# Two-layer diffusion backbone on one core: layer 1's modulation moved from the first attention units into the output projection of layer 0

## The chip, the cores and the metric

The kernel runs on one core of a Trainium2 chip, in one launch. A core has five engines, each with its own queue of instructions that it works off in order: TensorE (PE; matmuls, with the weight loads shown as PEld), VectorE (DVE), ScalarE (ACT), GpSimd (POOL) and SyncE (SP, which here only issues DMAs). Matmuls read SBUF and write banks of PSUM. Instructions of different engines wait for one another by semaphores. The metric is the device time of one execution in microseconds, as the median of several runs.

## What is computed

A latent stream of 1024 tokens and a context of 256 tokens, both 1024 wide, go through two layers. Layer 0 ("even") has global attention with grouped queries and windowed attention; layer 1 ("odd") has a convolution module and neighbourhood attention. Each layer starts with a modulation, which is what the change is about:

```python
def modulation(cond, w, b):
    m = jax.nn.silu(cond) @ w + b
    return jnp.split(m, 3, axis=-1)
...
    for i in range(DEPTH):
        sh_l, sc_l, g_l = modulation(c, mod_w[i], mod_b[i])
        sh_c, sc_c, g_c = modulation(c_ctx, mod_w[i], mod_b[i])
        h_lat = rms_norm(x_lat, norm_g[i]) * (1.0 + sc_l[:, None, :]) + sh_l[:, None, :]
        h_ctx = rms_norm(x_ctx, norm_g[i]) * (1.0 + sc_c) + sh_c
        ...
        x_lat = x_lat + g_l[:, None, :] * y_lat
        if update_ctx:
            x_ctx = x_ctx + g_c * y_ctx
```

`mod_w[i]` is 1024 x 3072 in fp32, 12.6 MB for each layer. Its three parts of 1024 columns give shift (part 0), scale (part 1) and gate (part 2). Layer 0's shift and scale are needed before its first projection, its gate at the output projection of layer 0. Layer 1's shift and scale are needed where layer 0's output is normed for layer 1, its gate at the very end, for the latent tokens alone.

## The kernel before

**Matmuls.** All products are fp32 in accuracy: each operand is split into a high and a low half, and a product is three matmuls (`mm3`, L319 to L322). Weights are split as they arrive (`load_w`, L326): a DMA from SyncE (`wr`, L331), a cast on ScalarE (`wh`, L298) and a subtraction on GpSimd or VectorE (`wl`, L301).

**Layer 0.** Its heads are cut into four units, and the attention runs over them in the order 2, 3, 0, 1, each with ten blocks of queries. For a block: loads of the queries (`QH`, `QL`, L565), score matmuls for the row maxima (`mx`, L578, L590, L598) with VectorE reducing them (`mp`, L580, L591, L599), the negative maximum (`nmt`, L379) and its transpose (`trn`, L389) that VectorE writes into the queries (`QL`, L390), then score matmuls (`st`, L467, L471), exponentials on ScalarE (`pf`, L479), their split into `ph` (ScalarE, L298) and `pl` (GpSimd, for a part VectorE, L301), the products with the values (`ov`, L411 to L413), and the finish on VectorE (`r`, `rb`, `y`, L421 to L635), with the gate `gt` (L569) and the result stored to `Od` (L638).

**What runs beside the attention.** `weave` (L497) interleaves attention steps with fill steps. While a unit's attention runs, the fill is the projections of the next one (`pq`, `trk`, `pg`, with rotary on VectorE in `rt` and `pc`). The first unit's projections have no attention beside them; this stretch is called solo. During the last unit (number 1) the fill is the output projection: `out0_part` for the heads of the first two units of the order, then of the third one (`po`, TensorE; at the end of each product the update of `x` by the gate of layer 0 on VectorE, L1012, called x update below, 24 for each of these parts), with its inputs loaded by `load_oh` (`hl` from `Od`, L991). Then follow the last unit's share of it (`final_proj`) and the norm for layer 1 (`norm_h`).

**Order.** Nothing is ordered by hand: a scheduler gives each instruction the priority at which the program emits it, and `later(LATE)` (L266, `LATE` = 100) puts those inside it a little later than their place. The result is a fixed order for each engine.

**Modulation.** `mod_half_v` (L195) makes 512 columns of a part for one or both conditions. The silu of the condition stands in `csil`, one value for each row of weights. For each of the eight blocks of 128 rows of `mod_w`, the weights (128 x 512 fp32, 256 KB) are scaled by `csil` and added to an accumulator `macc` of 128 x 512: for the first block by one tensor_scalar on VectorE (L216), for the others by one scalar_tensor_tensor on VectorE (L221), or, for three of the blocks of the context condition (`MODP`, not in solo), by a product on ScalarE (L218) and an add on GpSimd (L219). At the end four matmuls with a column of ones sum each accumulator over the partitions (`trm`, L227), and VectorE adds the bias (`modT`, L228) and, for the scale, makes `gs` (L232). Layer 1 takes 80 such accumulate steps: six half parts for two conditions would make twelve accumulators, but the gate is made for one condition only, which leaves ten, of eight steps each.

`mod_steps` (L851) runs through layer 0's gate and then all of layer 1. One step of it, the weights' load with the accumulates, is taken at every tick of the projections in solo (`TICK0` = 1, loads of 512 KB into key and value buffers not yet in use) and at every third tick afterwards (`TICK1` = 3, loads of 256 KB into two `mw` buffers), so that layer 1's modulation runs in solo and beside the first two attention units.

## Time and profile before

| | us |
|---|---|
| runs | 1563.86, 1567.05, 1573.72 |
| median of the runs | 1567.05 |
| profiled execution, its span on the page | 1569.6 |
| projections of the first unit (solo) | 45 to 160 |
| attention units with layer 1's modulation | 160 to 440 |
| output projection, first two parts, beside the last unit | 701 to 836 |
| its last part and the norm | 836 to 932 |

The profiled execution lies within the runs; the page shows nothing outside its span. The stretches are read from the trace, by the first and last instructions of the lines named above. Only a wait on the engine that bounds a stretch costs time there.

### The profile page before, as it was taken

Reading aid. Unit: us, or ns where it says so; the run is one execution under the profiler, and the core shown is the slowest. Engines: PE = TensorE matmul, PEld = TensorE weight load, DVE = VectorE, ACT = ScalarE, POOL = GpSimd, SP = SyncE. Lnnn points to the kernel's source line nnn. Section 1 sums busy time; section 2 is a strip of 40 time slices with the busy share of each in tenths; the row PEclk is TensorE's granted clock in tenths of the full one; section 3 lists DMA queues with packets and bytes.
Section 4 is the critical chain, followed back from the end, with each engine's and each line's share of the span. In section 5 each row is a group of like instructions: output and inputs, shape, how many; then the busy total and the mean of one; then the engine's idle time right before and its main releaser. Section 6 shows DMA issues by size and latency. Waiting matters only on the chain.

```text
span 1569.6 us, 22251 instructions
## 1 busy us (share of the span) xinstructions
PE 1460.8 (93%) x6984; PEld 1178.9 (75%) x6984; DVE 1129.4 (72%) x2172; ACT 762.0 (49%) x1545; POOL 830.0 (53%) x762
## 2 busy tenths in 40 slices
PE   6989999998999999899999889999999999899995
PEld 1878877876888677588887568888887787677784
DVE  4898896797768677455488668999654466776776
ACT  2721354545454754655555746443343445545472
POOL 1561463555465675756545756665443333444575
PEclk9899999999999999999999989999999999799897
DMA  9548245424431225612112022214547888889632
GB/s 337 190 142 260 87 142 167 132 67 125 154 116 47 67 91 167 224 47 61 48 38 85 14 94 61 81 58 148 177 154 224 237 229 242 248 231 251 187 95 108
DMA packets 199438, 221.03 MB, mean 141 GB/s; under 512 B 18956, under 2 KB 155352, under 8 KB 199320
## 3 DMA queue, kind: packets, MB, share of 16 engines
q1 hardware_dynamic: 192656, 208.04, 43.5%
q10 hardware_dynamic: 6664, 11.57, 2.3%
q8 instruction: 55, 0.90, 0.2%
q14 instruction: 63, 0.52, 0.1%
HBM read 159.51 MB, written 60.03 MB: 140 GB/s over the span
## 4 chain that ended last, share of the span: by engine, by line
PE 65%; DVE 14%; DMA 11%; issue 4%; POOL 2%; SPq 2%; ACT 1%; ACTq 0%; DVEq 0%; POOLq 0%
PE p L322 6%; PE p L321 6%; PE p L320 6%; PE ov L411 4%; PE ov L413 4%; PE ov L412 4%; PE po L320 4%; PE po L321 4%; PE po L322 4%; PE st L467 4%; PE st L471 4%; DMA mw<-in_mod_w_dram 3%; DVE macc L221 2%; PE pq L322 2%; PE pq L321 2%
## 5 line engine op out<-in xcount | busy, mean ns | idle before, releaser
L301 POOL TENSOR_TENSOR pl<-pf,ph 128x512 fp32r<-128x512 f32 (+4 forms) x321 | 393.7, 1237 | 320.1 <-ACT ph L298 260.0
L301 POOL TENSOR_TENSOR wl<-wr,wh 128x256 fp32r<-128x256 f32 (+2 forms) x256 | 197.5, 788 | 203.1 <-ACT wh L298 192.4
L479 ACT ACTIVATE pf<-st 128x512 f32<-128x512 f32 x284 | 167.3, 597 | 177.4 <-PE st L471 138.3
L298 ACT CAST ph<-pf 128x512 fp32r<-128x512 f32 (+4 forms) x364 | 210.5, 588 | 28.9 <-PE ov L412 21.5
L298 ACT CAST wh<-wr 128x256 fp32r<-128x256 f32 (+2 forms) x264 | 102.8, 404 | 172.9 <-DMA wr<-in_ev_qkv_dram 40.4
L320 PE MATMUL p<-hh,wh 128*128 128x512 f32 x448 | 177.5, 398 | 2.9 <-DVE spk L301 1.5
L321 PE MATMUL p<-hl,wh 128*128 128x512 f32 x448 | 178.0, 398 | 0.2 <-POOL hl L301 0.2
L322 PE MATMUL p<-hh,wl 128*128 128x512 f32 x448 | 175.9, 400 | 0.1
L467 PE MATMUL st<-QH,KAt 128*128 128x512 f32 (+4 forms) x364 | 145.4, 401 | 11.4 <-ACT pf L479 9.7
L411 PE MATMUL ov<-ph,Vt 128*128 128x512 f32 (+4 forms) x364 | 143.5, 394 | 9.7 <-ACT ph L298 5.0
L413 PE MATMUL ov<-pl,Vt 128*128 128x512 f32 (+4 forms) x364 | 144.1, 396 | 6.8 <-POOL pl L301 3.6
L471 PE MATMUL st<-QL,KBt 68*128 68x512 f32 (+4 forms) x364 | 139.0, 391 | 5.8 <-DVE QL L390 5.7
L412 PE MATMUL ov<-ph,Vt 128*64 128x512 f32 (+4 forms) x364 | 140.5, 386 | 0.0
L1122 DVE SCALAR_TENSOR_TENSOR cps<-U,taps,cps 128x512 f32<-128x512 f32 x184 | 124.3, 748 | 0.0
L591 DVE TENSOR_REDUCE mp<-mx 128x1 f32<-128x512 f32 x128 | 85.7, 682 | 42.5 <-PE mx L590 41.8
L221 DVE SCALAR_TENSOR_TENSOR macc<-mw,csil,macc 128x512 f32<-128x512 f32 x107 | 94.5, 901 | 17.5 <-DMA mw<-in_mod_w_dram 16.7
L320 PEld LDWEIGHTS p<-hh,wh 128*128 128x128 f32 x448 | 84.6, 189 | 23.6 <-DVE spk L301 1.7
L321 PEld LDWEIGHTS p<-hl,wh 128*128 128x128 f32 x448 | 84.5, 189 | 20.4 <-POOL hl L301 0.6
L322 PEld LDWEIGHTS p<-hh,wl 128*128 128x128 f32 x448 | 84.8, 189 | 20.1 <-POOL wl L301 0.6
L467 PEld LDWEIGHTS st<-QH,KAt 128*128 128x128 f32 x364 | 71.2, 196 | 33.4 <-ACT pf L479 17.6
L413 PEld LDWEIGHTS ov<-pl,Vt 128*128 128x128 f32 x364 | 71.1, 195 | 32.5 <-POOL pl L301 7.8
L411 PEld LDWEIGHTS ov<-ph,Vt 128*128 128x128 f32 x364 | 71.3, 196 | 27.3 <-ACT ph L298 8.4
(277 smaller groups left out, 3546.2 us busy)
## 6 DMA issues: line engine op xcount, KB each, us to landing
mw<-in_mod_w_dram SPq DMA_DIRECT2D x34, 512.0 KB, 5.9
Q<-qs SPq DMA_DIRECT2D x40, 256.0 KB, 2.7
QH<-Q SPq DMA_DIRECT2D x80, 128.0 KB, 2.8
wr<-in_od_d_dram SPq DMA_DIRECT2D x64, 128.0 KB, 2.7
mw<-in_mod_w_dram SPq DMA_DIRECT2D x28, 256.0 KB, 3.3
wr<-in_ev_qkv_dram SPq DMA_DIRECT2D x32, 192.0 KB, 3.6
KAt<-KD SPq DMA_DIRECT2D x16, 384.0 KB, 6.2
wr<-in_od_wo_dram SPq DMA_DIRECT2D x48, 128.0 KB, 3.2
```

The costliest lines, as they stand in the source:

```text
L221: VE.scalar_tensor_tensor(t, w, csil[:, dk, q : q + 1], t, op0=ALU.mult, op1=ALU.add)
L298: SC.copy(hi, src)
L301: (GP if leng == "g" else VE).tensor_tensor(lo, src, hi.bitcast(F32), op=ALU.subtract)
L320: PE.matmul(o, lh, rh, start=first, stop=False)
L321: PE.matmul(o, lh, rl, start=False, stop=False)
L322: done[0] = PE.matmul(o, ll, rh, start=False, stop=last)
L411: PE.matmul(o, V[:, 64:192], ph[:, :n], start=(t == 0), stop=False)
L412: PE.matmul(g.ov[0:64, q0 : q0 + n], V[:, 0:64], ph[:, :n], start=False, stop=False)
L413: pvs.append(PE.matmul(o, V[:, 64:192], pl[:, :n], start=False, stop=(last and g.sink is None)))
L467: sts.append(PE.matmul(st[:, :n], KA[:, cs], g.QH[:, q0 : q0 + n], start=True, stop=False))
L471: PE.matmul(st[:, :n], KB[0:68, cs], g.QL[0:68, q0 : q0 + n], start=False, stop=True)
L479: SC.activation(pf[:, :n], st[:, :n], AF.Exp, scale=1.0 if g.bias else SCALE)
```

## The change

Layer 0's gate alone stays in `mod_steps`, at every second tick of solo, and what is left of it is run before solo ends. Layer 1's modulation moves into `mod1_steps`, in the stage of the output projection. Its weights come in 48 loads of 256 KB into five slices of 128 x 512 in turn: two in a spare key buffer (`mwk`), three in a spare value buffer (`mwv`), both free once the attention of the third unit has ended. The accumulators take two buffers (`acc1`, `sq1`) that are otherwise used later, and ScalarE's product gets a buffer of its own (`mtmp`). The parts run in the order scale, shift, gate. One step is taken at each yield of `out0` for the first two of its three parts, under `later(LATE)`, and what is left is run ahead of `final_proj`. 68 of the 80 accumulate steps are on VectorE, 12 on ScalarE and GpSimd.

```diff
-TICK0, TICK1 = (1, 3)
+TICK0, TICK2 = (2, 1)
...
-    def mod_half_v(pool, l, part, j, conds):
+    def mod_half_v(l, part, j, conds, acc, slices=None, tmp=None):
...
-            if solo[0] and dk % 2 == 0:
-                w2 = mw_tile()
...
+            if slices is None:
+                if not pre:
+                    w2 = mw_tile()
...
             else:
-                w = pool.tile([P, 512], F32, tag="mw", name=nm("mw"), bufs=MWB)
+                w = slices()
                 SY.dma_start(w, a["mod_w"][l, dk * P : (dk + 1) * P, c0 : c0 + 512])
...
-                elif dk in MODP[q] and not solo[0]:
-                    SC.activation(w, w, AF.Identity, scale=csil[:, dk, q : q + 1])
-                    GP.tensor_tensor(t, t, w, op=ALU.add)
+                elif dk in MODP[q] and slices is not None:
+                    m = tmp()
+                    SC.activation(m, w, AF.Identity, scale=csil[:, dk, q : q + 1])
+                    GP.tensor_tensor(t, t, m, op=ALU.add)
...
         def tick():
             beat[0] += 1
-            if beat[0] % (TICK0 if solo[0] else TICK1) == 0:
+            if solo[0] and beat[0] % TICK0 == 0:
                 with later(LATE):
-                    if mark[0] is None or solo[0]:
-                        next(mods, None)
-                    else:
-                        with tc.issue_after(mark[0].ins):
-                            next(mods, None)
+                    next(mods, None)
...
         def mod_steps():
-            for part in (2,):
-                for j in range(2):
-                    yield from mod_half_v(ap, 0, part, j, (0, 1))
-            for part in range(3):
-                for j in range(2):
-                    yield from mod_half_v(ap, 1, part, j, (0, 1) if part < 2 else (0,))
+            for j in range(2):
+                yield from mod_half_v(0, 2, j, (0, 1), lambda: ap.tile([P, 512], F32, tag="macc", name=nm("macc"), bufs=2))
...
+        run(mods)
         solo[0] = False
...
-        run(mods)
...
+        sp_k = a0.tile([P, NTOK], F32, tag="KB", name=nm("mwk"), bufs=2)
+        sp_v = a0.tile([P, 1920], F32, tag="V", name=nm("mwv"), bufs=2)
+        spare = [t[:, i * 512 : i * 512 + 512] for t, k in ((sp_k, 2), (sp_v, 3)) for i in range(k)]
+
+        def mod1_steps():
+
+            def acc():
+                macc[0] += 1
+                tag = ("acc1", "sq1")[macc[0] % 2]
+                return op_.tile([P, 512], F32, tag=tag, name=nm("macc"), bufs=1)
+
+            def slices():
+                spare.append(spare.pop(0))
+                return spare[-1]
+
+            macc = [0]
+            for part in (1, 0, 2):
+                for j in range(2):
+                    yield from mod_half_v(1, part, j, (0, 1) if part < 2 else (0,), acc, slices,
+                                          lambda: op_.tile([P, 512], F32, tag="mtmp", name=nm("mtmp"), bufs=1))
+
+        mods1 = mod1_steps()
...
         def out0(fs, e, c, wh, wl):
...
             for f in fs:
                 mm3(pp[:, :n], wh[f][:, es], wl[f][:, es], oh[c][0][:, f, :], oh[c][1][:, f, :], f == fs[0], f == fs[-1])
                 if f % 2 == 1:
+                    if fs != final:
+                        with later(LATE):
+                            next(mods1, None)
                     yield
...
+        run(mods1)
         fp = [final_proj(c) for c in range(3)]
```

The order that the scheduler gives changes at three places that matter below. In the listings, a row has the line, the operation, what is written and read (the names of the program with a number for the tile), and the shape. Lines of the changed kernel differ: L220 there is L221 before, L214 is L216, L227 is L228, L1025 is L1012, L590 is L591, L579 is L580, L598 is L599, L564 is L565, L637 is L638, L330 is L331, L211 is L213.

VectorE near the first row maxima of the attention, before; `macc` are the accumulators of the modulation, `mp` the row maxima, `rt` and `pc` the rotary of the next unit:

```order
L580 TENSOR_REDUCE mp_1320<-mx_1326 128x2
L221 SCALAR_TENSOR_TENSOR macc_1218<-mw_1219,csil,macc_1218 128x512
L221 SCALAR_TENSOR_TENSOR macc_1218<-mw_1243,csil,macc_1218 128x512
L828 TENSOR_TENSOR rt_331_1769<-pc_1602,k_cs 128x320 x2
L599 ISA mx_1339,mp_1320<-mx_1339,k_bm 128x256
L599 ISA mp_1320 128x1
L830 TENSOR_TENSOR pc_1602<-pc_1602,k_cs 128x2x320
L221 SCALAR_TENSOR_TENSOR macc_1218<-mw_1305,csil,macc_1218 128x512
L599 ISA mx_1342,mp_1320<-mx_1342,k_bm 128x256
```

And in the changed kernel, at the first row maxima:

```order
L579 TENSOR_REDUCE mp_1225<-mx_1227 128x2
L579 TENSOR_REDUCE mp_1225<-mx_1231 128x2
L300 TENSOR_TENSOR qs_1059<-trk_1055,qs_1059 128x384
L227 TENSOR_TENSOR modT_90<-trm_1106,modb 128x4
L598 ISA mx_1244,mp_1225<-mx_1244,k_bm 128x256
L598 ISA mp_1225 128x1
L598 ISA mx_1247,mp_1225<-mx_1247,k_bm 128x256
L598 ISA mp_1225 128x1
L341 SCALAR_TENSOR_TENSOR sg_1214<-sg_1214,pg_1184 128x256
```

The accumulates have left the place between the row maxima; only the last bias add of layer 0's gate is still there.

VectorE in the second part of the output projection, from its 25th x update on, before; `x` are the updates, `mp` the row maxima of the last unit's attention:

```order
L1012 SCALAR_TENSOR_TENSOR x_1883_7455<-po_8599,modT_90,x_1883_7455 128x256
L591 TENSOR_REDUCE mp_7952<-mx_8073 128x1
L1012 SCALAR_TENSOR_TENSOR x_1892_7482<-po_8616,modT_90,x_1892_7482 128x512
L591 TENSOR_REDUCE mp_7952<-mx_8079 128x1
L1012 SCALAR_TENSOR_TENSOR x_1901_7508<-po_8640,modT_90,x_1901_7508 128x512
L591 TENSOR_REDUCE mp_7952<-mx_8099 128x1
L1012 SCALAR_TENSOR_TENSOR x_1883_7455<-po_8670,modT_90,x_1883_7455 128x256
```

The same place in the changed kernel, from the 26th x update on:

```order
L1025 SCALAR_TENSOR_TENSOR x_1836_7249<-po_8595,modT_90,x_1836_7249 128x512
L220 SCALAR_TENSOR_TENSOR macc_7761<-mwv_7208,csil,macc_7761 128x512
L220 SCALAR_TENSOR_TENSOR macc_7760<-mwk_7207,csil,macc_7760 128x512
L1025 SCALAR_TENSOR_TENSOR x_1845_7275<-po_8621,modT_90,x_1845_7275 128x512
L590 TENSOR_REDUCE mp_7824<-mx_8002 128x1
L220 SCALAR_TENSOR_TENSOR macc_7760<-mwv_7208,csil,macc_7760 128x512
L220 SCALAR_TENSOR_TENSOR macc_7761<-mwk_7207,csil,macc_7761 128x512
L590 TENSOR_REDUCE mp_7824<-mx_8019 128x1
L220 SCALAR_TENSOR_TENSOR macc_7760<-mwv_7208,csil,macc_7760 128x512
L1025 SCALAR_TENSOR_TENSOR x_1827_7222<-po_8653,modT_90,x_1827_7222 128x256
L220 SCALAR_TENSOR_TENSOR macc_7761<-mwk_7207,csil,macc_7761 128x512
```

Between two x updates there now stand one or two accumulates, and row maxima of the attention stand behind them. Up to the 25th x update there are 29 accumulates on VectorE, from there to the 45th 35, and 4 behind.

SyncE behind the loads of the last unit's third group of queries (`Q_4`), before; `Od` is the attention's result, `hl` the input of the output projection, `wr` its weights:

```order
L565 DMA QH_7180<-Q_4_113 64x2x256 x2
L565 DMA QL_7181<-Q_4_113 64x2x256
L638 DMA Od<-y_7273 128x2x128
L569 DMA gt_7722<-G_148 128x2x128
L991 DMA hl_7507<-Od 128x2x512
L331 DMA wr_8291<-in_ev_wo_dram 128x256
L331 DMA wr_8297<-in_ev_wo_dram 128x256
```

And in the changed kernel:

```order
L564 DMA QH_6945<-Q_4_113 64x2x256 x2
L564 DMA QL_6946<-Q_4_113 64x2x256
L211 DMA mwk_7207<-in_mod_w_dram 128x512 x3
L211 DMA mwv_7208<-in_mod_w_dram 128x512 x3
L211 DMA mwk_7207<-in_mod_w_dram 128x512
L211 DMA mwv_7208<-in_mod_w_dram 128x512 x2
L330 DMA wr_8238<-in_ev_wo_dram 128x256
L211 DMA mwv_7208<-in_mod_w_dram 128x512
L330 DMA wr_8244<-in_ev_wo_dram 128x256
L637 DMA Od<-y_7038 128x2x128
```

Nine loads of modulation weights stand ahead of the projection's weights and of the next store of the attention's result.

More of the change, by code (lines that the diff above doesn't have):

```diff
@@ L51 @@
 PFB = 2
-MWB, WRB = 2, 2
+WRB = 2
 OHQ = 0
@@ L101, in tile_kernel @@
     turn = [0, 0]
-    mk, mwp, hold, layer = [0], [None], [0], [0]
+    mk, mwp, layer = [0], [None], [0]
     sts, pvs = [], []
@@ L193, in mod_half @@
                                     op0=ALU.add, op1=ALU.mult)
[L195 removed]
+    def mod_half_v(l, part, j, conds, acc, slices=None, tmp=None):
         c0 = part * 1024 + j * 512
[L198 to L199 removed]
+        accs = [acc() for _ in conds]
         pre = []
         for dk in range(DK):
[L202 to L208 removed]
+            if slices is None:
+                if not pre:
+                    w2 = mw_tile()
+                    d_ = SY.dma_start(w2, a["mod_w"][l, dk * P : (dk + 2) * P, c0 : c0 + 512].rearrange("(d p) n -> p d n", d=2))
+                    if mwp[0] is not None:
+                        mm0.append(d_)
+                    pre = [w2[:, 0, :], w2[:, 1, :]]
                 w = pre.pop(0)
[L210 removed]
             else:
[L212 removed]
+                w = slices()
                 SY.dma_start(w, a["mod_w"][l, dk * P : (dk + 1) * P, c0 : c0 + 512])
@@ L714, in tile_kernel @@
                 elif ev == "v":
-                    run(mod_half_v(st0, 0, *mh.pop(0), (0, 1)))
+                    run(mod_half_v(0, *mh.pop(0), (0, 1), lambda: kvp.tile([P, 512], F32, tag="QH", name=nm("macc"), bufs=3)))
                 elif ev == "b":
@@ L876, in tile_kernel @@
             pass
+        run(mods)
         solo[0] = False
-        while hold[0]:
-            next(mods)
         assert not tails
```

8 lines of the change are left out of this document (removed).

## The prediction

> **What bounds the kernel now.** I read the page first: the span, the busy shares of the engines, and the chain that ended last.
>
> ```profile
> span 1569.6 us, 22251 instructions
> PE 1460.8 (93%) x6984; PEld 1178.9 (75%) x6984; DVE 1129.4 (72%) x2172; ACT 762.0 (49%) x1545; POOL 830.0 (53%) x762
> PE 65%; DVE 14%; DMA 11%; issue 4%; POOL 2%; SPq 2%; ACT 1%; ACTq 0%; DVEq 0%; POOLq 0%
> ```
>
> TensorE is busy for 93% of the span and makes up 65% of the chain, so the time is TensorE's work, plus the stretches in which it stands idle or runs at a lower clock. The changed kernel issues the same number of matmuls. It can win only idle time and clock that TensorE loses now, and lose by making it wait elsewhere. So the next view is the busy time by stretches, each with the granted clock (1.00 is full speed).
>
> ```profile
> core 0: us, PE busy (x) PEld busy (x) DVE busy (x) ACT busy (x) POOL busy (x), PEclk, DMA share, GB/s
> 45.00:107.00 62.00, 53.35 (x296) 50.54 (x295) 57.76 (x83) 31.02 (x65) 39.55 (x31) 0.92 0.42 136
> 107.00:160.00 53.00, 51.22 (x294) 46.21 (x292) 45.74 (x73) 11.30 (x25) 13.46 (x13) 0.97 0.82 256
> 160.00:300.00 140.00, 133.03 (x693) 112.29 (x694) 113.99 (x247) 63.06 (x146) 69.18 (x59) 0.98 0.45 137
> 300.00:440.00 140.00, 130.16 (x650) 107.66 (x650) 114.84 (x249) 65.23 (x146) 76.14 (x61) 0.98 0.37 113
> 701.00:772.00 71.00, 71.00 (x346) 57.73 (x345) 36.45 (x70) 36.39 (x68) 41.40 (x37) 1.00 0.16 47
> 772.00:823.00 51.00, 51.00 (x246) 41.32 (x245) 39.11 (x74) 26.08 (x48) 27.13 (x23) 1.00 0.16 47
> 823.00:836.00 13.00, 13.00 (x61) 10.29 (x60) 9.06 (x14) 7.30 (x14) 7.17 (x6) 1.00 0.12 38
> 836.00:932.00 96.00, 85.23 (x363) 63.39 (x363) 73.92 (x123) 60.11 (x118) 62.12 (x58) 0.91 0.19 61
> 1000.00:1050.00 50.00, 50.00 (x216) 40.23 (x215) 47.07 (x73) 20.33 (x32) 27.17 (x25) 1.00 0.22 72
> ```
>
> 45 to 160 us is the projections of the first unit, 160 to 440 us the attention units in which layer 1's modulation runs now, 701 to 836 us the first two parts of the output projection, 836 to 932 us the last part of it with the norm. Where the work leaves, TensorE is idle for 140 − 133.03 + 140 − 130.16 = 16.8 us and has lost 0.02 × 280 = 5.6 us of clock. Where it arrives, TensorE is never idle and the clock is full; there VectorE is busy for 51% (36.45 of 71) and 77% (39.11 of 51).
>
> **What the change removes.** The waits of TensorE between 160 and 440 us, by who released it (total, times, longest):
>
> ```profile
> PE st L471 <- DVE QL L390: 5.7, 2, 4.5
> PE st L467 <- ACT pf L479: 4.0, 6, 1.4
> PE ov L411 <- DVE y L633: 1.8, 3, 1.1
> PE mx L578 <- DMA QH<-Q: 1.5, 1, 1.5
> PE mx L578 <- DVE mp L599: 0.8, 2, 0.4
> PE mx L598 <- DVE mp L580: 0.7, 2, 0.6
> PE pg L320 <- DVE sg L342: 0.7, 1, 0.7
> PE trn L389 <- DVE nmt L379: 0.6, 1, 0.6
> PE mx L598 <- DVE mp L599: 0.5, 2, 0.3
> ```
>
> VectorE released 5.7 + 1.8 + 0.8 + 0.7 + 0.7 + 0.6 + 0.5 = 10.8 us of the 16.8. Is it the accumulates that made it late? For the longest wait, VectorE's timeline says yes (start, duration, then idle time before it and what ended that):
>
> ```profile
> 370.47 0.75 DVE L221 SCALAR_TENSOR_TENSOR macc<-mw,csil,macc 128x512 f32<-128x512 f32 x1 [1.52 <-DMA mw<-in_mod_w_dram]
> 376.37 0.75 DVE L221 SCALAR_TENSOR_TENSOR macc<-mw,csil,macc 128x512 f32<-128x512 f32 x1 [0.35 <-DMA mw<-in_mod_w_dram]
> 384.37 0.75 DVE L221 SCALAR_TENSOR_TENSOR macc<-mw,csil,macc 128x512 f32<-128x512 f32 x1 [0.93 <-DMA mw<-in_mod_w_dram]
> 385.15 0.68 DVE L390 TENSOR_TENSOR QL<-trn,k_bd 12x512 fp32r<-12x512 f32 x1
> ```
>
> Three accumulates stand in VectorE's queue ahead of the QL for which TensorE waited 4.5 us. They run for 3 × 0.75 = 2.25 us and hold the queue for 1.52 + 0.35 + 0.93 = 2.80 us more, waiting for their 256 KB of weights: 5.05 us, more than the wait. This one should vanish. Of the other 10.8 − 4.5 = 6.3 us I take two thirds, 4.2, since the accumulates are there but so is the rest of VectorE's queue, which stays 81% busy now ((113.99 + 114.84) of 280) and 67% without them (below). So 8.7 us. Clock that returns with them, in proportion to the idle time: 5.6 × 8.7 / 16.8 = 2.9. Gain 11.6 us. Its ends: 6 (the 4.5 us and a quarter of the 6.3) and all of 16.8 + 5.6 = 22.
>
> In 107 to 160 us at most 53 − 51.22 = 1.8 us of idle time and 0.03 × 53 = 1.6 of clock can be had, although VectorE is at 86% there; I take nothing. In 45 to 107 us the accumulates of layer 0 stay where they were in VectorE's order: nothing. The 512 KB loads that leave 107 to 160 us free the DMA engines (0.82 busy), for which TensorE does not wait there.
>
> The accumulates, as groups (busy, mean ns, then idle time before them), with the spread of the vector one (fastest, median and slowest in ns):
>
> ```profile
> L221 DVE SCALAR_TENSOR_TENSOR macc<-mw,csil,macc 128x512 f32<-128x512 f32 x36 | 34.7, 968 | 13.9 <-DMA mw<-in_mod_w_dram 13.6
> L216 DVE TENSOR_SCALAR macc<-mw,csil 128x512 f32<-128x512 f32 x5 | 2.4, 479 | 0.0
> L219 POOL TENSOR_TENSOR macc<-macc,mw 128x512 f32<-128x512 f32 x5 | 6.8, 1357 | 3.8 <-ACT mw L218 2.9 <-DVE gs L232 0.8
> L218 ACT ACTIVATE mw<-mw,csil 128x512 f32<-128x512 f32 x5 | 3.6, 724 | 11.3 <-DVE macc L221 11.3
> L227 PE MATMUL trm<-one,macc 128*128 128x2 f32 x40 | 4.9, 236 | 0.0
> L221 DVE SCALAR_TENSOR_TENSOR macc<-mw,csil,macc x36: 740/752/1842, 159.4 to 439.6; 128x512 f32<-128x512 f32 x36
> ```
>
> Leaving, they take 34.7 + 2.4 = 37.1 us of VectorE with them, which makes the 67% ((228.8 − 37.1 − a few small ones) of 280).
>
> **What the change adds.** In the output projection 68 accumulates on VectorE (10 tensor_scalar and 58 scalar_tensor_tensor), 12 products on ScalarE and 12 adds on GpSimd. By the order, 29 of the 68 (5 + 24) come before the 25th x update, 35 (5 + 30) between the 25th and the 45th, and 4 behind. Two rows set the pace of that place now:
>
> ```profile
> DVE mp L591 <- PE mx L590: 19.4, 11, 4.4
> DVE x L1012 <- PE po L322: 18.5, 11, 4.6
> L591 DVE TENSOR_REDUCE mp<-mx 128x1 f32<-128x512 f32 x36 | 24.4, 684 | 19.6 <-PE mx L590 19.4
> 697.44 1.24 SPq L565 DMA_DIRECT2D QH<-Q  x2
> ```
>
> The first two are VectorE's waits between 701 and 836 us: VectorE stands and waits for TensorE there, 38 us of it, so the cover exists. The question is whether it suffices in each stretch.
>
> - 772 to 823 us: VectorE 39.11 + 30 × 0.968 + 5 × 0.479 = 70.5, less four reduces that the new order puts behind the stretch (4 × 0.684 = 2.7): 67.8 us. TensorE has 51 us and takes over the transposes of five accumulators, 40 matmuls in the group above, 4.9 us: 56. VectorE becomes the bound, and the stretch grows by 67.8 − 56 = 12 us. The transposes are no loss against before, since they left another place.
> - 701 to 772 us: VectorE 36.45 + 24 × 0.968 + 5 × 0.479 = 62 us, TensorE 71 us and the transposes of three more accumulators (3 us), so 62 of 74, 84%. That load is nearest to 160 to 300 us, where VectorE is at 81% and TensorE idle for 5%: 0.05 × 71 = 3.5 us.
> - 823 to 836 us: four accumulates, 3.9 us, in 13 − 9.06 us of free time: nothing.
> - 836 to 932 us: the accumulates are done; between 0 and 3 us for what was pushed there. I take 0.
> - ScalarE (12 × 0.724 = 8.7 us) and GpSimd (12 × 1.357 = 16.3) stay at 58% and 68% (78.5 and 92 of 135): beside other work, nothing.
> - SyncE issues 48 loads of 256 KB. The first stands right behind the Q load of 697 us, and nine of them ahead of the projection's next weight load. Its slice comes free with the last attention matmul of the unit before, and the sixth load and all later ones wait until VectorE and ScalarE have released a slice. DMA engines are 0.16 busy there, so only SyncE's queue can hurt: weights of the projection, y and gate loads wait behind a mod_w load that waits for a slice. As VectorE keeps up until the dense stretch, I take nothing; it lies inside the range.
>
> So 12 + 3.5 = 15.5 us of idle time, and clock: 0.02 lost over 140 us of such running, as in 160 to 440 us, 2.7 us. Cost 18.2. Its ends: 10 (accumulates at the median of 0.752 instead of 0.968 take 30 × 0.216 = 6.5 off the dense stretch, and half of the clock goes with them: 18.2 − 6.5 − 1.4) and 24 (the 3 us behind 836 and the four reduces come on top: 18.2 + 3 + 2.7).
>
> On the clock, the trace has two dips of the same depth (stretch, busy times, clock), and the longest wait ahead of the first:
>
> ```profile
> 195.50:202.30 6.80, 4.76 (x12) 2.42 (x11) 6.63 (x17) 3.21 (x10) 4.20 (x4) 0.50 0.25 77
> 386.60:393.40 6.80, 6.42 (x25) 4.97 (x23) 6.04 (x13) 5.67 (x16) 5.74 (x6) 0.50 0.39 122
> PE st L467 <- ACT pf L479: 1.6, 2, 1.4
> ```
>
> The second follows the 4.5 us wait. The first follows waits of at most 1.4 us, so short waits close together can cost clock too; I keep the 2.7. [...]
>
> **Sum.** 18.2 − 11.6 = +6.6 us on the profiled execution: 1569.6 + 6.6 = 1576.2. The page shows nothing around the span, and the span is 2.55 us above the median of the runs, 1567.05, so in runs: 1573.7, say 1574. With gain 6 to 18 and cost 10 to 24 around it, the forecast's own range is 1567.05 − 18 + 10 = 1559 to 1567.05 + 24 − 6 = 1585.
>
> **The rivals.**
>
> *Accumulates and subtracts hold each other up (slower).* The vector accumulate's mean depends on GpSimd's load:
>
> ```profile
> L221 DVE SCALAR_TENSOR_TENSOR macc<-mw,csil,macc 128x512 f32<-128x512 f32 x44 | 35.6, 828 | 4.7 <-DMA mw<-in_mod_w_dram 4.2
> ```
>
> That is 107 to 160 us, GpSimd 25% busy (13.46 of 53): 828 ns. At 52% ((69.18 + 76.14) of 280) it is 968, with single ones of 1842, about one GpSimd instruction longer than the median. In the output projection GpSimd would be at 68%. If an accumulate there meets a subtract in two cases of three and waits half of one (0.65 us), it takes 0.752 + 0.42 = 1.17; 58 × 0.2 = 11.7 us more of VectorE, and GpSimd's subtracts, which feed the attention, wait in turn. With 2.4 us of clock: 1574 + 14 = 1588, up to 1598 if nearly every one waits. It decides from a mean of about 1.1 us. Against it: VectorE has slack before the dense stretch. [...]
>
> *The cover holds (faster).* In 107 to 160 us VectorE is at 86% and TensorE idle for 1.8 us; in 1000 to 1050 us VectorE is at 94% (47.07 of 50) and TensorE idle for nothing. So a loaded VectorE need not stop TensorE. Accumulates may slide into VectorE's 38 us of waits, and the dense stretch spread over its neighbours: cost 2, gain 18: 1567 + 2 − 18 = 1551, and 1547 with the gain's upper end of 22. Against it: the vector work of those two stretches has few results that an attention step waits for, as the maxima L591 are waited for here, and the order puts the 35 where it puts them.
>
> *The change does little at the start (R3).* The waits of 160 to 440 us pass on to ScalarE's exponentials (4.0 us already) or to Q loads: gain 3, cost 18: 1582.
>
> **How the numbers follow.** Forecast 0.44, hold-up 0.24, cover 0.22, little at the start 0.10. A measurement of this kernel tells about 1% from no change: 1551.4 and 1582.7. The forecast's range puts 0.03 above, the rest within. Hold-up: 0.21 above, 0.03 within. Cover: 0.13 below, 0.09 within. R3 lies on the bound: 0.05 each. Faster 0.13, within 1% 0.58, slower 0.29. Most of the chance is spread over both signs, so the range runs from the cover's best to the hold-up's worst, 1547 to 1598; beyond it stay what I did not think of.
>
> **What would show it.** In the profile of the changed kernel: the 4.5 us wait for QL gone and TensorE's idle time between the first row maxima and the second unit down from 16.8 to about 8; VectorE's accumulates in the output projection at a mean near 0.97 us (above 1.1: the hold-up); TensorE idle for some 15 us there, released by VectorE (maxima, x updates), most of it around the 25th to 45th x update, none (the cover) or spread evenly with GpSimd as the releaser (the hold-up); no TensorE wait on weight loads or gates behind SyncE's queue. I am wrong if the first units stay as idle as they are, if the output projection stays without a gap, or if a weight load of the projection is what TensorE waits for.

## The result, and the profile after

| | median us | range | runs | ratio to before, 95% interval |
|---|---|---|---|---|
| before | 1567.05 | 1559.22 to 1575.45 | 19 | |
| changed | 1577.13 | 1570.59 to 1581.08 | 19 | 1.0063, 1.0046 to 1.0081 |

The changed kernel is slower by 0.63%, some 10 us. The profiled execution has a span of 1575.8 us, 6.2 above the one of before; both lie within the runs of their kernel. From the page of the changed kernel, the span, the busy shares and the chain by engine:

```profile
span 1575.8 us, 22303 instructions
PE 1465.9 (93%) x6984; PEld 1181.4 (75%) x6984; DVE 1135.9 (72%) x2165; ACT 767.1 (49%) x1552; POOL 847.0 (54%) x769
PE 61%; DVE 17%; DMA 13%; issue 3%; POOL 2%; ACT 2%; SPq 1%; ACTq 0%; DVEq 0%; POOLq 0%
```

TensorE's share of the chain went from 65% to 61%, VectorE's from 14% to 17%. To see where the time came and went, both executions are cut at the same two matmuls: the 38th of the output projection, which stands ahead of the first moved accumulate, and the first of layer 1's projections. The columns are those of the busy times by stretch in the prediction. Before:

```profile
0.00:668.80 668.80, 613.51 (x3028) 497.51 (x3029) 507.63 (x974) 319.65 (x657) 357.72 (x297) 0.96 0.47 148
668.80:929.40 260.60, 249.83 (x1154) 196.71 (x1153) 173.13 (x302) 145.36 (x272) 152.32 (x135) 0.97 0.17 51
929.40:1569.60 640.20, 597.51 (x2805) 484.64 (x2804) 448.61 (x896) 296.98 (x617) 319.93 (x332) 0.96 0.57 170
```

And the changed kernel:

```profile
0.00:649.60 649.60, 605.13 (x2948) 493.92 (x2949) 451.53 (x885) 316.83 (x652) 348.68 (x292) 0.95 0.42 133
649.60:938.60 289.00, 266.77 (x1235) 206.56 (x1233) 235.42 (x384) 151.75 (x284) 179.20 (x146) 0.96 0.28 88
938.60:1575.80 637.20, 593.99 (x2805) 480.90 (x2805) 448.97 (x897) 298.52 (x618) 319.12 (x333) 0.96 0.57 172
```

| stretch | length | TensorE idle | TensorE busy |
|---|---|---|---|
| up to the moved accumulates | −19.2 | −10.8 (55.3 to 44.5) | −8.4 |
| output projection | +28.4 | +11.4 (10.8 to 22.2) | +16.9 |
| layer 1, which the change does not touch | −3.0 | +0.5 | −3.5 |
| sum | +6.2 | +1.1 | +5.0 |

So the first units won 19 us, and the output projection lost 28. The 80 matmuls that sum the moved accumulators over the partitions (9.8 us of TensorE's time in the changed kernel; called transposes, as in the prediction) went from the first row of the table to the second and cancel.

In the first units, the stretches and the waits of TensorE (148 to 414 us, the attention units that were 160 to 440 us before):

```profile
148.00:290.00 142.00, 141.71 (x756) 125.01 (x755) 84.73 (x201) 69.38 (x155) 65.61 (x59) 1.00 0.36 112
290.00:414.00 124.00, 121.11 (x625) 101.92 (x624) 104.53 (x230) 59.24 (x137) 71.85 (x58) 1.00 0.35 107
```

```profile
PE mx L597 <- DVE mp L598: 1.1, 1, 1.1
PE st L470 <- DVE QL L389: 0.7, 2, 0.4
PE trk L835 <- DVE qs L300: 0.6, 1, 0.6
PE trn L388 <- DVE nmt L384: 0.2, 1, 0.2
```

16.8 us of idle time have become 3.2, and the clock is full, though this stretch holds 1379 matmuls against 1342 before, 40 of which were transposes. The wait of 4.5 us for QL is gone. So are the waits that the profile of before had put down to ScalarE and to a query load; whether a late VectorE stood behind those is not shown.

The stretches on either side did not gain. Ahead of the attention and behind it, before and then in the changed kernel:

```profile
45.00:160.00 115.00, 104.56 (x587) 96.76 (x586) 103.50 (x155) 42.33 (x90) 53.01 (x43) 0.94 0.60 191
440.00:668.80 228.80, 215.14 (x1015) 172.20 (x1014) 153.46 (x278) 133.44 (x245) 153.09 (x123) 0.97 0.37 115
```

```profile
45.00:148.00 103.00, 91.44 (x478) 84.09 (x479) 83.72 (x129) 40.15 (x88) 52.72 (x43) 0.87 0.44 143
414.00:649.60 235.60, 221.37 (x1010) 174.82 (x1010) 157.10 (x281) 132.89 (x243) 152.16 (x122) 0.94 0.37 114
```

TensorE's idle time there went from 10.4 to 11.6 us and from 13.7 to 14.2, and the clock from 0.94 to 0.87 and from 0.97 to 0.94.

In the output projection, the stretches and the waits:

```profile
682.00:744.00 62.00, 60.57 (x302) 48.85 (x301) 49.35 (x76) 33.51 (x60) 44.48 (x36) 1.00 0.37 114
744.00:790.00 46.00, 42.48 (x202) 33.00 (x201) 45.63 (x78) 17.43 (x33) 25.55 (x20) 0.96 0.41 123
790.00:845.00 55.00, 47.89 (x208) 35.41 (x208) 53.79 (x81) 23.68 (x46) 27.69 (x20) 0.91 0.33 103
845.00:890.00 45.00, 41.77 (x178) 30.98 (x178) 34.73 (x64) 26.42 (x49) 28.58 (x23) 0.96 0.21 70
```

```profile
PE po L319 <- DVE x L1025: 7.7, 7, 2.4
PE ov L412 <- POOL pl L300: 3.6, 2, 3.2
PE st L466 <- ACT pf L478: 3.1, 6, 1.2
PE ov L410 <- DVE y L632: 2.0, 3, 1.4
...
PE trm L226 <- DVE modT L227: 1.5, 1, 1.5
PE mx L589 <- DVE mp L590: 0.9, 1, 0.9
PE trm L226 <- DVE macc L220: 0.7, 1, 0.7
```

From 744 to 845 us VectorE is busy 98% of the time (45.63 + 53.79 of 101), TensorE idles 3.5 + 7.1 us and its clock falls to 0.91. What TensorE waits for most is the x update (7.7 us in seven waits), in which VectorE reads the product's bank of PSUM and so sets it free for a later product.

How long the moved accumulates took: the groups between 680 and 850 us (busy, mean ns, idle before), then the fastest, median and slowest of each, and of the first accumulate of each accumulator (tensor_scalar, which has one 128x512 operand in SBUF and no second):

```profile
L220 DVE SCALAR_TENSOR_TENSOR macc<-mwv,csil,macc 128x512 f32<-128x512 f32 x34 | 37.4, 1106 | 1.5 <-DMA mwv<-in_mod_w_dram 1.2
L590 DVE TENSOR_REDUCE mp<-mx 128x1 f32<-128x512 f32 x36 | 24.0, 679 | 3.0 <-PE mx L589 2.8
L220 DVE SCALAR_TENSOR_TENSOR macc<-mwk,csil,macc 128x512 f32<-128x512 f32 x24 | 22.6, 944 | 0.3
L1025 DVE SCALAR_TENSOR_TENSOR x<-po,modT,x 128x512 f32<-128x512 f32 x28 | 20.6, 740 | 3.6 <-PE po L321 3.5
...
L1025 DVE SCALAR_TENSOR_TENSOR x<-po,modT,x 128x256 f32<-128x256 f32 x13 | 6.2, 474 | 2.6 <-PE po L321 2.5
...
L300 POOL TENSOR_TENSOR pl<-pf,ph 128x512 fp32r<-128x512 f32 x48 | 68.6, 1441 | 37.6 <-ACT ph L297 31.9 <-PE po L321 4.8 <-PE st L466 0.7
```

```profile
L220 DVE SCALAR_TENSOR_TENSOR macc<-mwv,csil,macc x34: 706/948/1765, 688.2 to 842.6; 128x512 f32<-128x512 f32 x34
L220 DVE SCALAR_TENSOR_TENSOR macc<-mwk,csil,macc x24: 735/744/1814, 684.9 to 840.4; 128x512 f32<-128x512 f32 x24
L214 DVE TENSOR_SCALAR macc<-mwk,csil x5: 477/486/1444, 683.5 to 823.0; 128x512 f32<-128x512 f32 x5
L214 DVE TENSOR_SCALAR macc<-mwv,csil x5: 470/476/1072, 731.0 to 812.1; 128x512 f32<-128x512 f32 x5
```

58 accumulates took 60.0 us, 1.03 us each, though the fastest took 0.71. GpSimd's subtracts `pl` beside them took 1.44 us. In before they took 1.30 in the same part of the kernel (660 to 850 us):

```profile
L301 POOL TENSOR_TENSOR pl<-pf,ph 128x512 fp32r<-128x512 f32 x66 | 85.2, 1300 | 67.0 <-ACT ph L298 48.5 <-PE st L471 9.2 <-PE po L322 4.3
```

Laid over GpSimd's instructions in the trace, 34 of the 58 run with GpSimd busy for more than half of their time and take 1.24 us on average; 21 run with GpSimd idle and take 0.742. The ten tensor_scalars show the same: five with GpSimd busy for more than half of their time take 0.89 us on average, five with GpSimd idle 0.48. One place with GpSimd busy, on the timelines of VectorE, GpSimd and TensorE (start, duration, then the idle time before it and what ended it):

```profile
794.71 2.88 DVE L220 SCALAR_TENSOR_TENSOR macc<-mwv,csil,macc 128x512 f32<-128x512 f32 x2
797.52 0.74 DVE L1025 SCALAR_TENSOR_TENSOR x<-po,modT,x 128x512 f32<-128x512 f32 x1
```

```profile
794.47 0.90 POOL L300 TENSOR_TENSOR wl<-wr,wh 128x256 fp32r<-128x256 f32 x1
795.34 1.71 POOL L300 TENSOR_TENSOR pl<-pf,ph 128x512 fp32r<-128x512 f32 x1
```

```profile
798.31 0.79 PE L319 MATMUL po<-hh,wh 128*128 128x512 f32 x1 [2.40 <-DVE x L1025]
```

Two accumulates that would take 1.5 us at the 0.742 above take 2.88 beside two subtracts of GpSimd, one of which is stretched to 1.71. Behind the accumulates in VectorE's queue stands the x update, and TensorE waits 2.40 us for it.

### The profile page after: what moved, and what is told of

Read it like the earlier page. It is cut to its first block, busy times and chain, and to the rows that moved or that the text cites. A ratio compares the mean times of both kernels' runs of the same rounds, so it can differ in the third digit from the quotient of the medians.

```text
span 1575.8 us, 22303 instructions
## 1 busy us (share of the span) xinstructions
PE 1465.9 (93%) x6984; PEld 1181.4 (75%) x6984; DVE 1135.9 (72%) x2165; ACT 767.1 (49%) x1552; POOL 847.0 (54%) x769
## 4 chain that ended last, share of the span: by engine, by line
PE 61%; DVE 17%; DMA 13%; issue 3%; POOL 2%; ACT 2%; SPq 1%; ACTq 0%; DVEq 0%; POOLq 0%
PE p L320 6%; PE p L319 6%; PE p L321 6%; PE ov L412 4%; PE ov L410 4%; PE ov L411 3%; PE st L470 3%; PE st L466 3%; DVE macc L220 3%; PE po L319 3%; PE po L320 3%; PE po L321 3%; PE pq L321 2%; PE pq L320 2%; PE pq L319 2%
## 5 line engine op out<-in xcount | busy, mean ns | idle before, releaser
L300 POOL TENSOR_TENSOR pl<-pf,ph 128x512 fp32r<-128x512 f32 (+4 forms) x321 | 401.8, 1263 | 319.5 <-ACT ph L297 254.5
L590 DVE TENSOR_REDUCE mp<-mx 128x1 f32<-128x512 f32 x128 | 85.6, 681 | 29.3 <-PE mx L589 28.7
L319 PE MATMUL pq<-wh,hh 128*128 128x384 f32 x256 | 87.8, 343 | 0.0
```

Of the source, the lines that this page charges most:

```text
L300: (GP if leng == "g" else VE).tensor_tensor(lo, src, hi.bitcast(F32), op=ALU.subtract)
L319: PE.matmul(o, lh, rh, start=first, stop=False)
```

## The experiments

Three causes were set against one another. *Hold-up*: a vector accumulate and a GpSimd instruction that run at the same time lengthen each other. *Count*: VectorE simply has too much to do in the crowded stretch. *Queue*: the weight loads, waiting for their slices, hold back other loads on SyncE. Ratios are to the kernel before, from the same chip; 0.1% is 1.6 us. The rows come from several chips, on which before took 1565.0 to 1567.2, so ratios are compared and not medians.

| kernel | median us | ratio | 95% interval |
|---|---|---|---|
| changed | 1577.13 | 1.0063 | 1.0046 to 1.0081 |
| none | 1545.61 | 0.9859 | 0.9834 to 0.9885 |
| one_input | 1554.19 | 0.9914 | 0.9889 to 0.9938 |
| more_pool | 1580.67 | 1.0081 | 1.0056 to 1.0107 |
| split_solo | 1567.73 | 1.0007 | 0.9989 to 1.0025 |
| no_loads | 1579.14 | 1.0090 | 1.0067 to 1.0112 |
| no_pool | 1586.96 | 1.0129 | 1.0106 to 1.0151 |
| before_one_input | 1574.00 | 1.0056 | 1.0036 to 1.0076 |
| split_thin | 1575.74 | 1.0063 | 1.0041 to 1.0085 |
| after_swap | 1560.39 | 0.9965 | 0.9949 to 0.9981 |
| after_tiny | 1554.88 | 0.9928 | 0.9908 to 0.9948 |
| before_swap | 1563.44 | 0.9982 | 0.9964 to 1.0000 |
| before_tiny | 1556.85 | 0.9939 | 0.9915 to 0.9963 |

### none: what the work costs in either place

```diff
-        mods1 = mod1_steps()
+        for q in range(2):
+            VE.tensor_copy(modT[1][:, :, q], modb[:, 1, :])
+            VE.tensor_copy(gs[1][:, :, q], normg[:, 1, :])
+        mods1 = iter(())
```

> The changed kernel with layer 1's modulation left out altogether (loads, accumulates, transposes; layer 1 takes the bare bias and norm gain). It splits the change into a gain and a price. If the traces of before and after are read rightly, before minus this kernel is about 19 us (13.7 of idle time and lost clock and 5.4 of transposes in the first units), and after minus this kernel about 28 us (23 of idle time and clock, 5 of transposes in the output projection): 1548, ratio 0.988. If instead the forecast's terms hold (11.6 and 18.2, with 5 us of transposes on either side), 1550 as well, but with the output projection only 23 us shorter than in after and the first units no faster than in after less 2 us. If the first units of after still carry a price from elsewhere (R3), their stretch here is as long as in after and the total is above 1555.

0.9859: layer 1's modulation costs 1.41%, 22 us, in its old place, and 1.0063 − 0.9859 = 2.04%, 32 us, in its new one. Both are somewhat more than the 19 and 28 us that were expected from the traces. The run has an order of its own as well, from the output projection on.

### one_input: the second operand taken away in the source

```diff
+                elif slices is not None:
+                    VE.tensor_reduce(t[:, 0:1], w, axis=AX.X, op=ALU.add)
                 else:
                     VE.scalar_tensor_tensor(t, w, csil[:, dk, q : q + 1], t, op0=ALU.mult, op1=ALU.add)
```

> The changed kernel with the 58 vector accumulates of the output projection replaced by a row sum of the weights alone (one operand in SBUF instead of two, 0.68 us instead of 0.74 undisturbed), so layer 1's modulation is wrong while loads, transposes, number and order of instructions stay. If VectorE's own instruction count is the price: VectorE is 58 x 0.06 = 3.5 us shorter, the time falls by 3 to 5 us. If accumulates and GpSimd's subtracts hold each other up: the accumulates lose 58 x (1.04 - 0.68) = 21 us and the subtracts pl go back from 1.44 to 1.30 us; the time falls by 10 to 15 us, with x updates no longer late by more than 1 us.

1.5% faster than the changed kernel, more than the hold-up was expected to give. But the scheduler made another order for this source, on TensorE too: in the traces the first 3162 matmuls are the same, the next is another. So the run does not say how much is the hold-up; after_swap below does.

### before_one_input: the same in the old place

```diff
+                elif l == 1:
+                    VE.tensor_reduce(t[:, 0:1], w, axis=AX.X, op=ALU.add)
                 else:
                     VE.scalar_tensor_tensor(t, w, csil[:, dk, q : q + 1], t, op0=ALU.mult, op1=ALU.add)
```

> The kernel before with layer 1's vector accumulates (solo and first attention units) replaced by a row sum of the weights (one operand in SBUF; layer 1's modulation is wrong, loads and transposes stay). If the hold-up is also what they cost in their old place: 36 x (0.97 - 0.68) = 10 us less VectorE beside the attention and as much again in solo, and 8 to 14 us faster than before, 1554 to 1559. If their old price was their number and the wait for their loads in VectorE's queue, 2 to 4 us faster.

A miss for every theory: less work, and 0.56% slower than before. Here too the order changed, behind the first 515 matmuls. before_swap, with the same instructions in before's order, is at 0.9982, so the order alone is worth 0.74%, 12 us. That is as much as the whole change.

### more_pool and no_pool: accumulates moved between the engines

```diff
-MODP = ((), (1, 3, 6))
+MODP = ((2, 5), (1, 3, 6))
```

> The changed kernel with 12 more accumulates moved from VectorE to ScalarE and GpSimd (two of eight for each latent accumulator: 24 there, 44 + 12 on VectorE and so on to 56). If VectorE's load bounds the stretch, 12 x 1.0 us leave it: 6 to 10 us faster than after. If the two engines hold each other up, GpSimd's adds have two SBUF operands as well and block the vector ones that stay: within 3 us of after or slower, with pl above 1.5 us.

```diff
-MODP = ((), (1, 3, 6))
+MODP = ((), ())
```

> The changed kernel with all 80 accumulates on VectorE: 12 products on ScalarE and 12 adds on GpSimd become 12 vector accumulates. If VectorE's count is the price: 12 us more VectorE work in a stretch at 98%, 6 to 12 us above after's 1577. If the mutual hold-up is: an accumulate costs its 1.04 us on VectorE, but the 12 adds of 1.32 us that block VectorE are gone: within 4 us of 1577.

With 12 accumulates more on ScalarE and GpSimd nothing was won (1.0081 against 1.0063, within the intervals). With none there, 0.66% were lost, as the count would have it. That would mean that VectorE's load matters and that GpSimd's adds are not a free way out. But both runs have orders of their own, so neither carries the verdict.

### no_loads: SyncE's queue

```diff
-                SY.dma_start(w, a["mod_w"][l, dk * P : (dk + 1) * P, c0 : c0 + 512])
+                mk[0] += 1
+                if mk[0] <= 5:
+                    SY.dma_start(w, a["mod_w"][l, dk * P : (dk + 1) * P, c0 : c0 + 512])
...
+        mk[0] = 0
```

> The changed kernel with 43 of the 48 weight loads of the output projection left out (the accumulates read the first five blocks again and again, so layer 1's modulation is wrong). If SyncE's queue is part of the price (loads that wait there for a slice hold back query loads, gates and projection weights), the time falls by 5 us or more below after's 1577. If VectorE and GpSimd holding each other up is the price, nothing in that changes: within 4 us of 1577.

1.0090: no faster. The loads and their place in SyncE's queue cost nothing that can be seen, to the extent that an order of its own allows this to be said.

### split_solo and split_thin: part of the work left in the old place

```diff
-TICK0, TICK2 = (2, 1)
+TICK0, TICK2 = (1, 1)
...
+            for j in range(2):
+                yield from mod_half_v(1, 0, j, (0, 1), lambda: ap.tile([P, 512], F32, tag="macc", name=nm("macc"), bufs=2))
...
-            for part in (1, 0, 2):
+            for part in (1, 2):
```

> Shift of layer 1 (32 of the 80 accumulates) goes into the solo projections with one step at every tick, as before had it; scale and gate (48) stay in the output projection. By the traces the accumulates in solo cost before nothing (TensorE waits 19.7 us there before, 19.9 after), so most of the gain of 19 us stays, and the output projection loses the dense stretch: 28 x 48/80 less about 5 more = 12 us. Expected 1560, 15 us under after and 5 to 8 under before. If the solo stretch is bound by loads (DMA engines 0.82 busy there before), it grows by 5 to 10 us and this lies at before. If the place is what costs and not the count, it lies at after less 5 us.

split_thin takes the steps of the output projection at every second yield besides:

```diff
                     if fs != final:
-                        with later(LATE):
-                            next(mods1, None)
+                        beat1[0] += 1
+                        if beat1[0] % 2 == 0:
+                            with later(LATE):
+                                next(mods1, None)
```

> As split_solo, with the 36 steps that stay in the output projection taken at every second yield instead of every one, so that by the order they reach over 40 x updates instead of 30. If the crowded place is what costs: 4 to 6 us under split_solo's 1567.7, and below before. If each accumulate costs what it costs because GpSimd works beside it, wherever it stands: within 3 us of split_solo.

split_solo ties with before, 0.56% under the changed kernel: 32 accumulates fewer in the output projection. It was expected 5 to 8 us under before, so this is a miss: either those in solo are not free, or the order took the gain; the run can't tell. Spreading the rest out did not help: split_thin is 0.56% above split_solo. Neither theory had said slower. Both have orders of their own.

### after_swap and after_tiny: the hold-up and the count, in one and the same order

To keep the order, the accumulates are replaced after it is fixed. Each keeps its place, its waits and its signals; in the traces TensorE, VectorE, ScalarE and GpSimd work off the same order as in the kernel that it is compared with. It becomes a row sum of its weights, over all 512 columns (swap) or one (tiny), which reads one operand in SBUF:

```diff
+def swap(nc):
...
+            if i.name in SWAP:
+                src, dst = cut(i.ins[0], 512), cut(i.outs[0], 1)
+                L[k] = mybir.InstTensorReduce(op=ALU.add, axis=AX.X, name=i.name, engine=i.engine, debug=i.debug,
+                                              ins=[src], outs=[dst], sync_info=i.sync_info)
```

> As one_input, but the 58 accumulates are replaced after the order is fixed, so every engine has after's order, waits and instruction count, and only the second SBUF operand and 0.06 us of each are gone (layer 1's modulation is wrong). If VectorE and GpSimd holding each other up is the price: 58 x (1.04 - 0.68) = 21 us of VectorE in a stretch that is 98% busy, 10 to 18 us faster than after, 1559 to 1567. If one_input owes its 23 us to the other order that the scheduler made for it: at most 5 us faster than after, 1572 or more.

> As after_swap, with each of the 58 reading one column: the accumulates' time on VectorE is gone (58 x 0.06 us stay), order, loads, transposes and GpSimd's 12 adds stay. What lies between after_swap and this is the price of VectorE's own time, without the hold-up; what lies between this and none (1546) that of transposes, adds and order. If VectorE's time is the price by itself: another 8 to 12 us under after_swap, near 1552. If the hold-up is most of it: within 5 us of after_swap. If order and transposes are most of it: 1562 or more.

In after_swap: two crowded stretches of the output projection, the row sums' spread, GpSimd's subtracts (660 to 850 us), and the wait for the x update:

```profile
738.00:783.00 45.00, 43.86 (x219) 34.54 (x217) 43.82 (x85) 21.64 (x41) 25.69 (x23) 1.00 0.46 135
783.00:834.00 51.00, 46.79 (x219) 36.03 (x218) 43.31 (x77) 22.45 (x42) 23.22 (x19) 0.97 0.35 109
```

```profile
L221 DVE TENSOR_REDUCE macc<-mwv x34: 639/678/687, 683.5 to 824.3; 128x1 f32<-128x512 f32 x34
L221 DVE TENSOR_REDUCE macc<-mwk x24: 660/676/687, 680.7 to 822.4; 128x1 f32<-128x512 f32 x24
```

```profile
L303 POOL TENSOR_TENSOR pl<-pf,ph 128x512 fp32r<-128x512 f32 x58 | 75.1, 1304 | 42.6 <-ACT ph L300 37.3 <-PE po L324 4.9
```

```profile
PE po L322 <- DVE x L1028: 2.0, 3, 1.0
```

None of the 58 takes over 0.69 us, though GpSimd is busy for 57% and 46% of these two stretches (25.69 of 45, 23.22 of 51), the subtracts are back at 1.30, the waits for x updates fall from 7.7 to 2.0 us, and the kernel is 1.0063 − 0.9965 = 0.98% faster, 15 us, as was expected of the hold-up. Only 58 × 0.06 = 3.5 us of VectorE's time have another reason, the shorter instruction. A high share of VectorE alone did not stop TensorE here: from 738 to 783 us VectorE is still busy for 97%, and TensorE idles 1.1 us. What the run leaves open is which part of the accumulate meets GpSimd: a row sum has one operand less in SBUF, and it also writes one column instead of 512.

After_tiny takes off another 0.37%, 6 us: that is VectorE's own time for the 58. It falls between its two expectations (8 to 12, or within 5). What then lies between it and none, 0.69% or 11 us, is the rest: the loads, the ten tensor_scalars, transposes, ScalarE's products and GpSimd's adds, and the order.

### before_swap and before_tiny: the same in the old place

The same edit on the kernel before, 65 accumulates.

> The kernel before in its own order, with layer 1's vector accumulates (solo and first attention units) replaced by row sums after the order is fixed. If the hold-up costs in the old place what it costs in the new: 65 x 0.27 = 18 us of VectorE, of which TensorE waits for a third to a half, 4 to 9 us faster than before, 1558 to 1562. If VectorE has room for it there: within 3 us of before.

> As before_swap, each reading one column: VectorE's time for layer 1's accumulates gone in their old place. By the trace of before TensorE waits 10.8 us for VectorE there and loses 5.6 us of clock: 10 to 16 us faster than before, 1551 to 1556, with the wait for QL of 4.5 us shorter but for the loads that VectorE still waits for (2.8 us of it). If the old price was transposes and order: less than 6 us.

0.9982 and 0.9939: the hold-up costs 0.18% in the old place, 3 us, VectorE's own time 0.43%, 7 us, and the rest down to none 0.80%, 13 us. For before_swap that is the expectation of an engine with room; before_tiny falls just short of the 10 to 16 us that its first expectation had. The wait for QL, in before_swap and then in before_tiny:

```profile
PE st L474 <- DVE QL L393: 5.2, 2, 4.6
```

```profile
PE st L474 <- DVE QL L393: 1.8, 1, 1.8
```

Without the accumulates' time 1.8 us of it are left. VectorE still waits for weights in its queue ahead of that QL, 2.1 us in three places of the 14 us before it; that these waits make up the 1.8 us is not shown.

The four runs in fixed orders and none give the price of the same 80 accumulates in the two places, in % of before's time (0.1% is 1.6 us):

| | old place | new place |
|---|---|---|
| hold-up, with the 0.06 us by which each row sum is shorter (swap) | 0.18 | 0.98 |
| VectorE's own time (swap to tiny) | 0.43 | 0.37 |
| the rest: loads, tensor_scalars, transposes, products, adds, order (tiny to none) | 0.80 | 0.69 |
| sum | 1.41 | 2.04 |

Each ratio has an interval of about 0.2% to either side, so the two rows in the middle can't be told apart between the places. The first can: the difference of 0.80% is more than the whole change, 0.63%. With row sums in both places the two kernels tie, 0.9965 against 0.9982.

## Why the prediction was right, point by point

**The bound and the two terms.** TensorE's waits carried the change, as said. With 8 us of transposes taken out on both sides, as the prediction did, the first units won 19.2 − 8 = 11.2 us against the forecast 11.6, and the output projection lost 28.4 − 8 = 20.4 against 18.2 (with the 9.8 us that the transposes took, 9.4 and 18.6). That both terms come this near is in part luck: within each, idle time and clock missed in opposite directions, as the next two points show. The sum at the end of layer 0 is 9.2; the profiled execution gave 3.0 back in layer 1, where nothing changed, and the medians of 19 runs stand 10 apart, against 6.6 to 7 forecast.

**The gain.** More idle time left the attention units than forecast (13.6 us against 8.7), since the waits for ScalarE and for a query load went as well. Some came back elsewhere, 10.8 us being left over all first units. And the clock of the first units as a whole did not rise (0.96 to 0.95), against a forecast gain of 2.9: it rose to 1.00 in the attention units and fell to 0.87 ahead of them and to 0.94 behind. The prediction had put the stretch ahead of the attention at nothing; why its clock fell is not shown. R3 falls, as nothing passed on to ScalarE. The reason given for the 4.5 us wait holds: it went with the change, and before_tiny brings it to 1.8.

**The cost.** The crowded stretch came where it was put, at 744 to 845 us of the new time, with VectorE at 98%, x updates as what TensorE waits for, and 10.6 us idle there against the 12 worked out. In the 62 us ahead of it 1.4 us were lost, against 3.5 in 71. Over the whole output projection idle time grew by 11.4 us against 15.5 forecast, and TensorE's busy time, without the transposes, by 7 to 9 against the 2.7 of clock. One bound is not the working's own: the forecast's range takes 18 for the upper end of the gain, which had been worked out as 22; with 22 it would begin at 1555, and the result lies inside either way.

**The hold-up** was the prediction's first rival, priced at 1588 and said to decide from a mean of 1.1 us. The mean was 1.03, and the rival's time did not come. Yet its mechanism is what makes the change lose, and that the forecast still came out near is luck in this respect: the forecast's own 0.968 us for an accumulate already held 0.22 us of hold-up over the median of 0.752, measured in the old place, where the hold-up costs 3 us, and used in the new one, where it costs 15. At the undisturbed time the prediction's lower end of the cost was 10; after_swap's output projection is 275.6 − 260.6 − 8 = 7 us longer than before's, near that end, and the kernel is then 0.35% faster than before. The step that I would now write otherwise is the separation of rival and forecast. Two things differ between the places. In the old one 30 of the 65 vector accumulates stood in solo, where they took 0.763 us on average; the other 35, in the attention units, met GpSimd about as often (17 over half covered, 1.21 us each) as those in the new place (34 of 58, 1.24 us). So the lengthening over the undisturbed time adds up to some 9 us of VectorE in the old place and 17 in the new. And these 9 us cost 3 us of time, the 17 cost up to 15. VectorE is 81% busy in the attention units and 98% from 744 to 845 us, so that there the lengthening ends in a wait of TensorE; this second part is argued from the waits, and no run varies VectorE's room alone.

The lengthening differs by instruction, in the same places of one order: the accumulates of the changed kernel took 0.71 to 1.81 us, the row sums of after_swap 0.64 to 0.69. A second operand of 128x512 in SBUF is not needed for it in these traces: the tensor_scalars of the changed kernel, with one, took 0.47 to 1.44 us.

**The cover** (the second rival) falls: VectorE's waits for TensorE did fill, from 38 us to 9 (2.8 + 3.5 + 2.5 in the groups of 680 to 850 us), but the crowded stretch had too few of them. That the stretches from which it was argued have vector work for which few attention steps wait, as the prediction held against it, was not tested.

**SyncE's loads** at nothing: no_loads bears it out, as far as a run with an order of its own can.

What stays open: how far the +10 us is owed to the order that the scheduler happened to make. With the same instructions, before_one_input and before_swap lie 12 us apart, and one_input and after_swap 8 us. The prices of the hold-up and of VectorE's own time stand, since they were taken in fixed orders; the rest and the two sums of the last table contain whatever their orders cost. A version that beats both kernels was not found; split_solo, the best of those that compute everything, ties with before.

## What to carry to other kernels

Before moving vector work beside other work, read from the trace how long each of its instructions takes with GpSimd idle and with GpSimd busy, and how busy GpSimd is in the new place. Here the accumulate with two 128x512 operands and the tensor_scalar with one were lengthened, the row sum was not. A mean from the old place carries the old place's share of this (here 0.968 us, against a median of 0.752). Then ask what waits for the engine: some 9 us of lengthening cost 3 us of time in one place and 17 us up to 15 in the other. When an experiment edits the source of a kernel whose order is made by a scheduler, compare the orders first; a change of one instruction can be worth more through the order than through itself, and replacing instructions after the order is fixed keeps the two apart.

## What the runs showed of the hardware that was not expected

An accumulate of 128 x 512 took 0.742 us with GpSimd idle and 1.24 on average with GpSimd busy for more than half of its time, and GpSimd's subtract grew from 1.30 to 1.44 us in turn. A tensor_scalar went from 0.48 to 0.89 us in the same way. A row sum of the same weights stayed at 0.69 or less with GpSimd busy for 46% to 57% of the stretch. The granted clock was 0.91 from 790 to 845 us, where the longest wait of TensorE was 2.40 us; the forecast had counted on 0.98.
